# Strassen's seven products for the first feed-forward product of a decoder layer

## The chip, the core and the metric

The kernel runs on one core of a Trainium2 chip: TensorE (PE) for matrix products, VectorE (DVE), ScalarE (ACT) and GpSimd (POOL) for elementwise work, SyncE (SP) for issuing the transfers between DRAM and the on-chip memory SBUF. Products land in PSUM, which has eight banks of 512 fp32 columns. The metric is the device time of one execution in microseconds (us), the median of several runs.

## The reference, cut to what matters

One decoder layer on 512 tokens of width 2048: an attention mixer, then the feed-forward part, then a gate with a per-layer embedding, and a last norm. The change is in the feed-forward part (and in how all weights from there on are staged).

```python
h = h + nsa_mixer(rms_norm(h, norm_mix[i]), ...)
hn = rms_norm(h, norm_ffn[i])                            # 512 x 2048
h = h + jnp.square(jax.nn.relu(hn @ ffn_w1[i])) @ ffn_w2[i]   # 2048 -> 8192 -> 2048
gate = jax.nn.sigmoid(rms_norm(h, norm_ple[i]) @ ple_w_gate[i])
h = h + (p[i] @ ple_w_proj[i]) * gate
return rms_norm(h, norm_final)
```

## The kernel before

All is kept transposed: features on the 128 partitions, the 512 tokens along the columns. `h` is 16 tiles of 128 x 512, held in SBUF from start to end.

**Precision.** Each fp32 operand is split in an upper part (fp16) and a lower part (the rest, fp16), and each product is three matmuls (`mm3`, L68): upper by upper, upper by lower, lower by upper. Every matmul (L66) is preceded by its weight load. Since fp16 has a small range, each weight unit is scaled by a power of two first.

**Weight units.** From the feed-forward part on, weights come in units of 128 x 2048 fp32 (1 MB). `unit16` (L687) loads one on SP's queue, sums its squares on ACT (`sum_sq`, L676, whose unwanted elementwise result goes into the buffer of the lower part, L692), takes the power of two (`scale_of`, L666: one 128x1 matmul to bank `s1`, then three tiny DVE operations, L671 to L673), and splits it by halves of 1024 columns (`scaled_split`, L680: upper on ACT, L684; lower on DVE, L685). Five split units fit (`w16`), and raw ones in three buffers (`rawt`, L79). `take(n, ahead)` (L711) hands out the next units and prepares four more ahead.

**Feed-forward.** 8192 inner features are 16 groups G of four blocks of 128. `up(G)` (L838) makes a group: for each block, one weight unit, 16 values of k, 3 matmuls of 512 columns into one bank (`gemm16`, L826), then relu and scale on DVE (L848), square on ACT (L850) and a sum of the squares for the next scale (L851). `squash` (L857) scales and splits the group's result. `down(G)` (L872) multiplies it by four units of the second weight, 4 x 4 output tiles of 4 x 3 matmuls each, and adds each to `h` on DVE (L883). The order is up 0, up 1, down 0, up 2, down 1, and so on. Four banks rotate (`gbank`, L785).

**Ahead of it** `norm_late` (L215) gives the norm's factor, `proj(0)` (L792) computes half of the embedding's projection into eight tiles `pj` that stay in SBUF until the gate, and `normed` (L807) scales and splits `h` into `xs`: per k one DVE scaling (L812), the upper part on ACT (L815), the lower on DVE (L816). `take_held` (L822) holds the next units back until the tenth k is split. **Behind it** come `proj(1)`, `normed` again, 16 gate units of the same shape (the last two by token halves, so by matmuls of 256 columns, L938), the last norm and the output tiles `fo` (L953).

**Order.** Instructions are written down in program order, and a planner orders each engine's queue when the program is built, with its own estimate of the times; on the chip every queue then runs strictly in that order, each instruction waiting for what it needs.

Of the kernel before, what the change touches and what calls it, by code (L numbers as in the profile page):

```python
# [7 lines left out]
F32 = mybir.dt.float32  # L8
# [20 lines left out]
HOLD = 9  # L29
EPS = 1e-6  # L30
# [6 lines left out]
def trunk_kernel(ctx, tc, xT, pT, gains, w_kcvc, w_blk, w_gates, w_out, w1c, w2c, posT,  # L37
# [8 lines left out]
    wraw = ctx.enter_context(tc.tile_pool(name="wraw", bufs=2))  # L46
    tmp = ctx.enter_context(tc.tile_pool(name="tmp", bufs=2))
    a_sb = ctx.enter_context(ExitStack())
    wsp = a_sb.enter_context(tc.tile_pool(name="wsp", bufs=3))
# [29 lines left out]
    def rawt(shape=(128, 2048), own=False):  # L79
        rawt.n += 1  # L80
        if own or (rawt.mix and rawt.n % 3 == 0):
            return P["raw2"].tile(list(shape), F32, name="raw", tag="raw")
        return wraw.tile(list(shape), F32, name="raw", tag="raw")

    rawt.n = 0
    rawt.mix = False
    P = {}

    def load(src, cols=2048, pieces=1, own=False):
        r = rawt(own=own)  # L90
# [575 lines left out]
    def scale_of(sq, n=1):  # L666
        p = bank("s1")
        mm(p[:, 0:n], wb[:, 0:128], sq, True, True)
# [18 lines left out]
    def unit16(src):  # L687
        r = load(src, own=not rawt.mix)
        hi = P["w16"].tile([128, 2048], F16, name="wh", tag="wh")
        lo = P["w16"].tile([128, 2048], F16, name="wl", tag="wl")  # L690
        sq = P["sm"].tile([128, 1], BF16, name="sq", tag="sq")
        sum_sq(lo.bitcast(BF16), r, sq)  # L692
        sc, inv = scale_of(sq)
        scaled_split(hi, lo, r, sc)
        return hi, lo, inv

    order = [w_proj[0]]
    for G in range(NG + 1):
        if G < NG:
            order += [ffn1[G * FG + j] for j in range(FG)]  # L700
        if G > 0:
            order += [ffn2[G - 1, c] for c in range(4)]
    order += [w_proj[1]] + [w_pg[m] for m in range(NK)]
    units = []
    taken = [0]

    def prep(n):
        while len(units) < min(len(order), n):
            units.append(unit16(order[len(units)]))

    def take(n=1, ahead=4):  # L711
        taken[0] += n
        prep(taken[0] + ahead)
        return units[taken[0] - n:taken[0]]

    def embed_in():
        px = [P["px"].tile([128, 2 * S], F16, name=f"px{e}", tag=f"px{e}") for e in range(2)]
        praw = load(pT, 1024, own=True)
        sqp = P["sm"].tile([128, 1], BF16, name="sq", tag="sq")
        sum_sq(px[1].bitcast(BF16), praw[:, 0:1024], sqp)  # L720
        psc, pinv0 = scale_of(sqp)
        P["pinv"] = pinv = P["keepc"].tile([128, 1], F32, name="pinv")
        DVE.tensor_copy(pinv, pinv0)
        scaled_split(px[0], px[1], praw[:, 0:1024], psc)
        P["pxs"] = px

    def early(n0, n1, gains=False):
        if gains:
            embed_in()
            yield  # L730
            gain_scales()
            yield
        for n in range(n0, n1):
            prep(n + 1)
            yield
# [18 lines left out]
    for hd in range(HEADS):  # L754
# [8 lines left out]
        elif hd + 2 < HEADS:  # L763
            merge([(pvg, 10), (s_stage(hd + 1, (pp, small)), 5)], n, fill)
        elif hd + 1 < HEADS:
            merge([(pvg, 10), (s_stage(hd + 1, (pp, small)), 5), (early(0, 1, True), 3)], n, fill)
        else:
            merge([(pvg, 10), (early(1, 3), 2)], n, fill)
        if hd == HEADS - 3:
            x_sb.close()  # L770
            for nm, bufs in (("sm", 6), ("keepc", 1), ("px", 1), ("w16", 5), ("raw2", 1)):
# [3 lines left out]
    merge([(early(3, 4), 2)], 16, fill)  # L775
    drain(fill)
    a_sb.close()
    rawt.mix = True
    pjp = pool("pjp")
    xp = pool("xp", side="left")  # L780
    wk = pool("wk", 4, side="left")
# [10 lines left out]
    def proj(q):  # L792
        hi, lo, inv = take(1, 3)[0]
        px = P["pxs"]
        iv = P["sm"].tile([128, 1], F32, name="iv", tag="iv")
        DVE.tensor_mul(iv, inv, P["pinv"])
        for m in range(8):
            o = gbank()
            for e in range(2):
                ws = slice(e * 1024 + m * 128, e * 1024 + (m + 1) * 128)  # L800
                xs = slice(e * S, (e + 1) * S)
                mm3(o, hi[:, ws], lo[:, ws], px[0][:, xs], px[1][:, xs], e == 0, e == 1)
            t = pjp.tile([128, S], F32, name="pj", tag=f"pj{q * 8 + m}")
            ACT.activation(t, o, AF.Copy, scale=iv)
            pj.append(t)

    def normed(i, rs):  # L807
        gx = P["gx"]
        xs = []
        for k in range(NK):  # L810
            t = wk.tile([128, S], F32, name="xt", tag="t")
            DVE.scalar_tensor_tensor(t, h[k], gx[:, i, k:k + 1], rs, op0=OP.mult, op1=OP.mult)  # L812
            a = xp.tile([128, S], F16, name="xh", tag=f"xh{k}")
            b = xp.tile([128, S], F16, name="xl", tag=f"xl{k}")
            ia = ACT.activation(a, t, AF.Copy)  # L815
            ib = DVE.tensor_sub(b, t, a)  # L816
            if k == HOLD:
                held[:] = ia, ib
            xs.append((a, b))
        return xs  # L820

    def take_held(n):  # L822
        with tc.issue_after(held[0].ins), tc.issue_after(held[1].ins):
            return take(n, 3)

    def gemm16(os, us, xs):  # L826
        for k in range(NK):
            for o, (hi, lo, _) in zip(os, us):
                ws = slice(k * 128, (k + 1) * 128)
                mm3(o, hi[:, ws], lo[:, ws], xs[k][0], xs[k][1], k == 0, k == NK - 1)  # L830
# [4 lines left out]
    with tc.tile_pool(name="ff", bufs=1) as ff:  # L835
        xs = normed(0, rs)

        def up(G, prev=None):  # L838
            fq = P["sm"].tile([128, FG], F32, name="fq", tag="fq")
            fj = ff.tile([128, S], BF16, name="fj", tag="fj")  # L840
            ts = []
            for j0, step in (((0, 2), (2, 1), (3, 1)) if G == 0 else ((0, 1), (1, 1), (2, 1), (3, 1))):
                us = take_held(step) if step == 2 else take(step)
                os = [gbank() for _ in us]
                gemm16(os, us, xs)
                for j, (o, u) in enumerate(zip(os, us), j0):
                    t = wk.tile([128, S], F32, name="ft", tag="t")
                    DVE.tensor_scalar(t, o, 0.0, u[2], op0=OP.max, op1=OP.mult)  # L848
                    t2 = ff.tile([128, S], F32, name="ft2", tag=f"t2{j}")
                    ACT.activation(t2, t, AF.Square)  # L850
                    ACT.activation(fj, t2, AF.Square, accum_out=fq[:, j:j + 1])  # L851
                    ts.append(t2)
                if prev and j0 == 0:
                    sqd.append(squash(*prev))
            return ts, fq
# [16 lines left out]
        def down(fs, fiv, last, prev=None):  # L872
            for c in range(4):
                hi, lo, inv = take()[0]
                iv = P["sm"].tile([128, 1], F32, name="iv", tag="iv")
                DVE.tensor_mul(iv, inv, fiv)
                for e in range(4):
                    m = 4 * c + e
                    o = gbank()
                    for j in range(FG):  # L880
                        ws = slice(j * 512 + e * 128, j * 512 + (e + 1) * 128)
                        mm3(o, hi[:, ws], lo[:, ws], fs[j][0], fs[j][1], j == 0, j == FG - 1)
                    DVE.scalar_tensor_tensor(h[m], o, iv, h[m], op0=OP.mult, op1=OP.add)  # L883
                    if last:
                        norm_sq(m, 12)
# [147 lines left out]
```

## Time and profile before

| | us |
|---|---|
| median of 3 runs | 2403.87 (2402.72 to 2404.31) |
| the profiled execution | 2402.69 |
| its span, first to last instruction | 2400.6 |
| TensorE busy in the span | 2367.3 (99%) |
| VectorE busy | 1303.8 (54%) |
| ScalarE busy | 1128.5 (47%) |
| mean granted clock of TensorE | 0.994 of full |

The span is one execution, and the rest of the profiled time lies around it. Busy time of TensorE says little by itself, since matmuls overlap: the listed duration of a 512-column matmul is about 380 ns, the distance from one start to the next about 216 ns. In the feed-forward part the kernel runs in groups that repeat every 83.10 us.

### The profile page before, as it was taken

How to read it: one execution, taken by the hardware profiler on the slowest of the kernel's cores; microseconds unless marked ns; L12 is line 12 of the kernel's file. 1: busy time of each engine (PE TensorE's matmuls, PEld its weight loads, DVE VectorE, ACT ScalarE, POOL GpSimd, SP SyncE). 2: the span in 40 equal slices, each digit the busy share in tenths (PEclk: the TensorE clock that was granted, in tenths of full speed). 3: DMA queues.
4: the chain of work that ended last, by engine and by line, in shares of the span. 5: the costliest groups of instructions: out<-in, count | busy, mean ns of one | idle time of the engine just before them, and what ended most of it. 6: DMA issues, size and time to landing. Idle time of an engine off the chain costs nothing.

```text
span 2400.6 us, 28596 instructions
## 1 busy us (share of the span) xinstructions
PE 2367.3 (99%) x11495; PEld 1406.4 (59%) x11495; DVE 1303.8 (54%) x2410; ACT 1128.5 (47%) x1638; POOL 328.9 (14%) x176
## 2 busy tenths in 40 slices
PE   8999999999999989999999999999999999999997
PEld 6888888888888744444444444444444444444445
DVE  6347656656556864554455445545544544555643
ACT  5324333333334566545445444544454454545751
POOL 4253233333323210000000000000000000002012
PEclk9999999999999999999999999999999999999998
DMA  5232122222222323323332233222332233322311
GB/s 196 95 123 71 53 71 71 71 71 71 71 71 79 123 71 123 104 90 106 106 106 90 103 105 106 97 98 104 106 105 95 100 105 105 102 92 88 108 69 71
DMA packets 35557, 227.35 MB, mean 95 GB/s; under 512 B 4320, under 2 KB 4704, under 8 KB 9568
## 3 DMA queue, kind: packets, MB, share of 16 engines
q1 hardware_dynamic: 35424, 225.53, 27.2%
q8 instruction: 90, 1.47, 0.3%
q14 instruction: 43, 0.35, 0.0%
HBM read 221.32 MB, written 4.19 MB: 94 GB/s over the span
## 4 chain that ended last, share of the span: by engine, by line
PE 96%; DVE 2%; issue 1%; ACT 0%; POOL 0%; DMA 0%; SPq 0%; DVEq 0%; POOLq 0%; ACTq 0%
PE g_ps L66 54%; PE pt_ps L66 32%; PE s_ps L66 5%; PE o_ps L66 3%; PE pt_ps L430 1%; DVE h L302 0%; DVE wl L685 0%; PE pt_ps L422 0%; DVE p L387 0%; DVE xt L812 0%; POOL raw L962 0%; DMA h<-in_xT_dram 0%; DVE al L168 0%; DVE nm L374 0%; DVE raw L964 0%
## 5 line engine op out<-in xcount | busy, mean ns | idle before, releaser
L66 PEld LDWEIGHTS <-wh 128*128 128x128 f16 x4736 | 461.9, 98 | 546.9 <-issue 6.6
L684 ACT ACTIVATE wh<-raw,sc 128x1024 f16<-128x1024 f32 x292 | 319.3, 1140 | 459.6 <-DVE sc L672 459.6
L685 DVE SCALAR_TENSOR_TENSOR wl<-raw,sc,wh 128x1024 f16<-128x1024 f32 x292 | 367.4, 1285 | 131.6 <-ACT wh L684 131.6
L66 PEld LDWEIGHTS <-wl 128*128 128x128 f16 x2368 | 231.5, 98 | 259.7 <-issue 3.9
L678 ACT ACTIVATE wl<-raw 128x2048 bf16<-128x2048 f32 x146 | 278.6, 1908 | 205.0 <-PE g_ps L66 123.6
L75 POOL TENSOR_TENSOR wl<-raw,wh 128x1024 fp32r<-128x1024 f32 x100 | 240.6, 2411 | 507.0 <-ACT wh L74 497.1
L182 POOL TENSOR_TENSOR ssacc<-ssacc,sq 128x512 f32<-128x512 f32 x50 | 73.8, 1477 | 1493.3 <-issue 1342.3
L66 PE MATMUL pt_ps<-xl,wh 128*128 128x512 f16 (+1 forms) x672 | 252.1, 375 | 2.2 <-DVE xl L816 2.2
L66 PE MATMUL pt_ps<-xh,wh 128*128 128x512 f16 (+1 forms) x672 | 249.8, 375 | 3.0 <-ACT xh L815 3.0
L66 PE MATMUL pt_ps<-xh,wl 128*128 128x512 f16 (+1 forms) x672 | 252.2, 375 | 0.0
L66 PE MATMUL g_ps<-xh,wh 128*128 128x512 f16 (+1 forms) x640 | 239.4, 374 | 0.0
L66 PE MATMUL g_ps<-xh,wl 128*128 128x512 f16 (+1 forms) x640 | 239.3, 374 | 0.0
L66 PE MATMUL g_ps<-xl,wh 128*128 128x512 f16 (+1 forms) x640 | 239.3, 374 | 0.0
L74 ACT ACTIVATE wh<-raw 128x1024 fp32r<-128x1024 f32 (+1 forms) x122 | 125.6, 1043 | 223.3 <-PE g_ps L66 159.7
L671 DVE TENSOR_SCALAR e<-s_ps 128x1 int32<-128x1 int32 x164 | 25.5, 155 | 354.1 <-PE s_ps L66 346.9
L66 PE MATMUL g_ps<-ah,wh 128*128 128x512 f32 x544 | 215.2, 396 | 0.0
L66 PE MATMUL g_ps<-ah,wl 128*128 128x512 f32 x544 | 214.0, 394 | 0.0
L66 PE MATMUL g_ps<-al,wh 128*128 128x512 f32 x544 | 212.7, 391 | 0.0
L883 DVE SCALAR_TENSOR_TENSOR h<-pt_ps,iv,h 128x512 f32<-128x512 f32 x128 | 96.0, 750 | 180.7 <-PE pt_ps L66 180.7
L66 PE MATMUL pt_ps<-fh,wl 128*128 128x512 f16 x512 | 194.0, 379 | 0.0
L66 PE MATMUL pt_ps<-fl,wh 128*128 128x512 f16 x512 | 194.0, 379 | 0.0
L66 PE MATMUL pt_ps<-fh,wh 128*128 128x512 f16 x512 | 194.0, 379 | 0.0
(243 smaller groups left out, 3627.0 us busy)
## 6 DMA issues: line engine op xcount, KB each, us to landing
raw<-in_ffn_dram SPq DMA_DIRECT2D x128, 1024.0 KB, 4.9
raw<-in_w_blk_dram SPq DMA_DIRECT2D x32, 1024.0 KB, 4.9
raw<-in_w_out_dram SPq DMA_DIRECT2D x16, 1024.0 KB, 4.8
raw<-in_w_pg_dram SPq DMA_DIRECT2D x16, 1024.0 KB, 4.9
h<-in_xT_dram SPq DMA_DIRECT2D x16, 256.0 KB, 6.6
raw<-in_w_kcvc_dram SPq DMA_DIRECT2D x4, 1024.0 KB, 4.9
raw<-in_w1c_dram SPq DMA_DIRECT2D x4, 1024.0 KB, 5.6
raw<-in_w_kcvc_dram SPq DMA_DIRECT2D x6, 512.0 KB, 6.6
```

The source lines that it names most:

```text
L66: nc.tensor.matmul(o, w, x, start=start, stop=stop, skip_group_check=True)
L74: ACT.activation(hi, src, AF.Copy)
L75: (eng or DVE).tensor_sub(lo, src, f32(hi))
L182: (DVE if e else POOL).tensor_add(acc[e], acc[e], sq)
L430: nc.tensor.transpose(pt[:, (i - kc) * 128:(i - kc + 1) * 128], A["P", hd, b, i, kc], ident)
L671: DVE.tensor_scalar(e[:, 0:n], p[:, 0:n].bitcast(I32), 24, None, op0=OP.logical_shift_right)
L678: ACT.activation(junk, src, AF.Square, accum_out=sq)
L684: ACT.activation(hi[:, cs], src[:, cs], AF.Copy, scale=sc)
L685: DVE.scalar_tensor_tensor(lo[:, cs], src[:, cs], sc, hi[:, cs], op0=OP.mult, op1=OP.subtract)
L883: DVE.scalar_tensor_tensor(h[m], o, iv, h[m], op0=OP.mult, op1=OP.add)
```

## The change

Blocks of the first feed-forward product are taken two at a time from group 2 on (`STD = 2`). The pair's weight (256 output features x 2048), the input (2048 x 512 tokens) and the result are each cut in 2 x 2 blocks, and the eight block products of the plain scheme are replaced by seven (Strassen's scheme in Winograd's form): each is 8 values of k, 3 matmuls, 256 columns. For that,

- `combos(k)` makes four sums of blocks of the input once, during groups 0 and 1, which stay on the plain scheme but with matmuls of 256 columns;
- `prepare` makes four sums of weight blocks for each pair (S1 to s4, on DVE), and splits seven pieces, not four;
- `up_pair` runs the products over four banks x, v, y, u; two banks take a second product on top of the first, after ACT has copied the first sum out (`keep`) or DVE has used it (`total`).

Weights are staged in pieces of 1024 columns: six raw buffers, nine slots of split pieces. `pump` is called after every product (`used`), stages a unit when its raw buffers are free by count, and splits one piece when a slot is free. Squares go quarter by quarter, with the unwanted result in PSUM, and `scale_of` sums the columns by one tiny matmul each. The first half of the projection is written to DRAM (`pjd`) and read back before the gate; the embedding is loaded and split twice. Buffers of the working tiles `wk` go from four to three, those of `fo` from three to two.

```diff
+RAWS = 6
+SLOTS = 9
+STD = 2
+H2 = S // 2
...
-        mm(p[:, 0:n], wb[:, 0:128], sq, True, True)
+        c = sq.shape[-1] // n
+        for x in range(c):
+            mm(p[:, 0:n], wb[:, 0:128], sq[:, x * n:(x + 1) * n], x == 0, x == c - 1)
...
+    PAIR = ("11", "12", "S2", "S1", "s3", "22", "s4")
+
+    def stage(it):
+        it.raw = []
+        if len(it.src) == 2:
+            quarters = [(it.src[a], b) for a, b in ((0, 0), (1, 0), (1, 1), (0, 1))]
+        else:
+            quarters = [(it.src[0], b) for b in range(need(it))]
+        ps4 = P["sm"].tile([128, 4], BF16, name="sq4", tag="sq4")
+        for x, (src, b) in enumerate(quarters):
+            r = P["raw"].tile([128, 1024], F32, name="raw", tag="raw")
+            nc.sync.dma_start(out=r, in_=src[:, b * 1024:(b + 1) * 1024])
+            sum_sq(sbank()[:, 0:1024], r, ps4[:, x:x + 1])
+            it.raw.append(r)
+        it.sc, it.inv = scale_of(ps4[:, 0:len(quarters)])
+
+    def slot(it, name, src):
+        hi = P["w16"].tile([128, 1024], F16, name="wh", tag="wh")
+        lo = P["w16"].tile([128, 1024], F16, name="wl", tag="wl")
+        scaled_split(hi, lo, src, it.sc)
+        it.w[name] = (hi, lo)
+
+    def prepare(it):
+        if len(it.src) == 1:
+            for b in range(need(it)):
+                slot(it, b, it.raw[b])
+                yield
+            return
+        a11, a21, a22, a12 = it.raw
+        for name in PAIR:
+            if name == "S2":
+                s1 = P["S"].tile([128, 1024], F32, name="S1", tag="S")
+                s2 = P["S"].tile([128, 1024], F32, name="S2", tag="S")
+                DVE.tensor_add(s1, a21, a22)
+                DVE.tensor_add(s2, s1, a11)
+            elif name == "s3":
+                s3 = P["S"].tile([128, 1024], F32, name="S3", tag="S")
+                DVE.tensor_add(s3, a11, a21)
+            elif name == "s4":
+                DVE.tensor_add(s2, s2, a12)
+            slot(it, name, {"11": a11, "12": a12, "22": a22}.get(name) or
+                 {"S2": lambda: s2, "S1": lambda: s1, "s3": lambda: s3, "s4": lambda: s2}[name]())
+            yield
+
...
+            items += [Item(ffn2[G - 1, c]) for c in range(4)]
+    items += [Item(pT), Item(w_proj[1])] + [Item(w_pg[m]) for m in range(NK)]
...
+    def pump():
+        while True:
+            n = st["staged"]
+            if n < min(len(items), st["limit"]) and st["raws"] + need(items[n]) <= RAWS:
+                stage(items[n])
+                st["raws"] += need(items[n])
+                st["staged"] += 1
+                continue
+            n = st["split"]
+            if n < st["staged"] and st["slots"] < SLOTS:
+                if st["gen"] is None:
+                    st["gen"] = prepare(items[n])
+                    st["left"] = 7 if need(items[n]) == 4 else need(items[n])
+                next(st["gen"])
+                st["slots"] += 1
+                st["left"] -= 1
+                if need(items[n]) == 4:
+                    st["raws"] -= {2: 2, 1: 1, 0: 1}.get(st["left"], 0)
+                else:
+                    st["raws"] -= 1
+                if st["left"] == 0:
+                    next(st["gen"], None)
+                    st["gen"] = None
+                    st["split"] += 1
+                continue
+            return
+
+    def used():
+        st["slots"] -= 1
+        pump()
+
...
+            for nm, bufs in (("sm", 12), ("keepc", 1), ("w16", SLOTS), ("raw", RAWS)):
...
+    P["S"] = pool("S", 2, side="left")
+    wk = pool("wk", 3, side="left")
+    pjd = tc.dram_tile([8, 128, S], F32, name="pjd")
...
+            else:
+                t = wk.tile([128, S], F32, name="pjt", tag="t")
+                ACT.activation(t, o, AF.Copy, scale=iv)
+                nc.sync.dma_start(out=pjd[m], in_=t)
+        for e in range(3):
+            used()
...
+    def held_pump(limit):
+        with tc.issue_after(held[0].ins), tc.issue_after(held[1].ins):
+            st["limit"] = limit
+            pump()
...
+                wh, wl = it.w[k // 8]
+                ws = slice(k % 8 * 128, (k % 8 + 1) * 128)
+                for x, (c0, n) in enumerate(widths):
+                    xh, xl = xs[k][x]
+                    mm3(o[:, c0:c0 + n], wh[:, ws], wl[:, ws], xh, xl, k == 0 and x == 0, k == NK - 1)
+            if k % 8 == 7:
+                for _ in its:
+                    used()
...
+            if k < 8:
+                a = [xp.tile([128, H2], F16, name=f"x1{c}", tag=f"x1{c}{k}") for c in "hl"]
+                b = [keep12[c][k // 2][:, k % 2 * H2:(k % 2 + 1) * H2] for c in range(2)]
+                xsplit(a[0], a[1], t[:, 0:H2])
+                xsplit(b[0], b[1], t[:, H2:])
+                xs.append([tuple(a), tuple(b)])
+                X["11", k] = tuple(a)
...
+        def combos(k):
+            ta, tb = xt(0, k, rs), xt(0, k + 8, rs)
+            cm = P["S"].tile([128, 4, H2], F32, name="cm", tag="S")
+            DVE.tensor_sub(cm[:, 0], ta[:, 0:H2], ta[:, H2:])
+            DVE.tensor_sub(cm[:, 2], tb[:, H2:], ta[:, H2:])
+            DVE.tensor_add(cm[:, 3], cm[:, 0], tb[:, H2:])
+            DVE.tensor_sub(cm[:, 1], cm[:, 3], tb[:, 0:H2])
+            a = [xp.tile([128, 4, H2], F16, name=f"xc{c}", tag=f"xc{c}{k}") for c in "hl"]
+            xsplit(a[0][:, 0:3], a[1][:, 0:3], cm[:, 0:3])
+            ACT.activation(a[0][:, 3], cm[:, 3], AF.Copy, scale=-1.0)
+            DVE.scalar_tensor_tensor(a[1][:, 3], cm[:, 3], -1.0, a[0][:, 3], op0=OP.mult, op1=OP.subtract)
+            for x, n in enumerate(("t1", "T4", "T3", "t2")):
+                X[n, k] = (a[0][:, x], a[1][:, x])
+
+        def squares(c, fq, j, ts):
+            t2 = ff.tile([128, S], F32, name="ft2", tag=f"t2{j}")
+            ACT.activation(t2, c, AF.Square)
+            sum_sq(sbank()[:, 0:S], t2, fq[:, j:j + 1])
+            ts.append(t2)
+
...
+        def up_pair(G, j0, fq, ts, hook):
+            it = take()
+            ninv = P["sm"].tile([128, 1], F32, name="ninv", tag="ninv")
+            DVE.tensor_scalar(ninv, it.inv, -1.0, None, op0=OP.mult)
+            z = {}
+            c = [wk.tile([128, S], F32, name="ft", tag="t") for _ in range(2)]
+            o = {}
+
+            def prod(b, w, x, first):
+                if first:
+                    o[b] = gbank()
+                wh, wl = it.w[w]
+                for k in range(8):
+                    ws = slice(k * 128, (k + 1) * 128)
+                    xh, xl = X[x, k]
+                    mm3(o[b][:, 0:H2], wh[:, ws], wl[:, ws], xh, xl, first and k == 0, k == 7)
+
+            def keep(n):
+                z[n] = wk.tile([128, H2], F32, name="z", tag="z")
+                ACT.activation(z[n], o["x"][:, 0:H2], AF.Copy)
+
+            def total(e, half, n, b):
+                DVE.tensor_add(c[e][:, half * H2:(half + 1) * H2], z[n], o[b][:, 0:H2])
+
+            prod("x", "11", "11", True)
+            keep(1)
+            used()
+            prod("v", "12", "21", True)
+            total(0, 0, 1, "v")
+            used()
+            prod("x", "S2", "t2", False)
+            keep(2)
+            used()
+            prod("y", "S1", "t1", True)
+            used()
+            hook(G, j0)
+            prod("x", "s3", "T3", False)
+            keep(3)
+            total(1, 1, 3, "y")
+            used()
+            prod("u", "22", "T4", True)
+            total(1, 0, 3, "u")
+            used()
+            prod("y", "s4", "22", False)
+            total(0, 1, 2, "y")
+            used()
+            for e in (1, 0):
+                DVE.tensor_scalar(c[e], c[e], ninv if e else it.inv, 0.0, op0=OP.mult, op1=OP.max)
+            for e in range(2):
+                squares(c[e], fq, j0 + e, ts)
...
+                if G == 0 and j0 >= 2:
+                    combos(j0 - 2)
+                if G == 1 and j0 < 3:
+                    combos(2 + 2 * j0)
+                    combos(3 + 2 * j0)
+
+            if G < STD:
+                up_std(G, fq, ts, hook)
+            else:
+                for j0 in (0, 2):
+                    up_pair(G, j0, fq, ts, hook)
...
+    P["pj"] = pool("pjp", side="left")
     proj(1)
+    xp = pool("xp2", side="left")
+    for m in range(8):
+        t = P["pj"].tile([128, S], F32, name="pj", tag=f"pj{m}")
+        nc.sync.dma_start(out=t, in_=pjd[m])
+        pj.insert(m, t)
...
-                fo = rawt((128, 8, HT))
+                fo = plx.tile([128, 8, HT], F32, name="fo", tag="fo")
```

## Rows read from the trace of the kernel before

**Rows 1.** The page: busy time by engine, and the chain's shares.
```profile
PE 2367.3 (99%) x11495; PEld 1406.4 (59%) x11495; DVE 1303.8 (54%) x2410; ACT 1128.5 (47%) x1638; POOL 328.9 (14%) x176
...
PE 96%; DVE 2%; issue 1%; ACT 0%; POOL 0%; DMA 0%; SPq 0%; DVEq 0%; POOLq 0%; ACTq 0%
```

**Rows 2.** Stretches: length, busy us (instructions) by engine, clock, DMA; group 1's up units; a steady group.
```profile
912.80:954.40 41.60, 41.60 (x199) 18.92 (x197) 19.39 (x38) 24.17 (x32) 0.00 (x0) 1.00 0.32 110
...
1079.10:1162.20 83.10, 83.10 (x394) 37.77 (x393) 40.77 (x74) 40.95 (x48) 0.00 (x0) 1.00 0.30 102
```

**Rows 3.** The chain in order of time: start, us, what, count; 512-column, then 256-column matmuls.
```profile
1085.12 10.38 PE pt_ps L66 x48
...
2361.89 10.49 PE g_ps L66 x96
```

**Rows 4.** Timeline of TensorE (start, us, instruction) around one scale matmul.
```profile
900.50 0.38 PE L66 MATMUL g_ps<-xl,wh 128*128 128x512 f16 x1
900.72 0.17 PE L66 MATMUL s_ps<-sq,wb 128*128 128x1 bf16 x1
900.75 0.38 PE L66 MATMUL g_ps<-xh,wl 128*128 128x512 f16 x1
```

**Rows 5.** Groups by line and shape, whole span: count, busy us, mean ns, idle before.
```profile
L66 PEld LDWEIGHTS <-wh 128*128 128x128 f16 x4736 | 461.9, 98 | 546.9 <-issue 6.6
L685 DVE SCALAR_TENSOR_TENSOR wl<-raw,sc,wh 128x1024 f16<-128x1024 f32 x292 | 367.4, 1285 | 131.6 <-ACT wh L684 131.6
L684 ACT ACTIVATE wh<-raw,sc 128x1024 f16<-128x1024 f32 x292 | 319.3, 1140 | 459.6 <-DVE sc L672 459.6
L678 ACT ACTIVATE wl<-raw 128x2048 bf16<-128x2048 f32 x146 | 278.6, 1908 | 205.0 <-PE g_ps L66 123.6 <-PE pt_ps L66 51.1 <-PE s_ps L66 27.8
...
L850 ACT ACTIVATE ft<-ft 128x512 f32<-128x512 f32 x64 | 39.1, 612 | 0.0
...
L812 DVE SCALAR_TENSOR_TENSOR xt<-h,gx,o_ps 128x512 f32<-128x512 f32 x32 | 22.4, 742 | 4.5 <-PE o_ps L66 4.5
...
L816 DVE TENSOR_TENSOR xl<-xt,xh 128x512 f16<-128x512 f32 x32 | 20.9, 685 | 2.3 <-ACT xh L815 2.3
...
L75 DVE TENSOR_TENSOR tl<-pt_ps,th 128x256 fp32r<-128x256 f32 x32 | 13.4, 418 | 21.7 <-ACT th L74 21.7
```

**Rows 6.** Waits over the span: who waited for whom, us, times, longest.
```profile
DVE e L671 <- PE s_ps L66: 346.9, 71, 5.3
...
DVE wl L685 <- ACT wh L684: 131.6, 126, 3.3
```

**Rows 7.** Timelines of ScalarE and TensorE: one unit's square, accumulator, scale matmul, upper half.
```profile
1079.11 1.91 ACT L678 ACTIVATE wl<-raw 128x2048 bf16<-128x2048 f32 x1 [1.74 <-PE g_ps L66]
1080.93 0.19 ACT L678 ACTIVATION_READ_ACCUMULATOR wl<-raw 128x1 bf16 x1
...
1084.95 0.17 PE L66 MATMUL s_ps<-sq,wb 128*128 128x1 bf16 x1
...
1085.57 2.19 ACT L684 ACTIVATE wh<-raw,sc 128x1024 f16<-128x1024 f32 x2 [4.46 <-DVE sc L672]
```

**Rows 8.** Timelines of ScalarE and VectorE where the feed-forward part begins.
```profile
863.20 0.69 ACT L804 ACTIVATE pj<-g_ps,iv 128x512 f32<-128x512 f32 x1 [1.41 <-PE g_ps L66]
...
865.64 2.72 DVE L812 SCALAR_TENSOR_TENSOR xt<-h,gx,o_ps 128x512 f32<-128x512 f32 x4 [1.31 <-PE o_ps L66]
```

**Rows 9.** DMA issues: count, KB each, median us from issue to landing.
```profile
raw<-in_ffn_dram SPq DMA_DIRECT2D x128, 1024.0 KB, 4.9
...
out_dram<-raw SPq DMA_DIRECT2D x3, 256.0 KB, 2.6
```

**Rows 10.** Timelines of GpSimd and VectorE at the output tiles.
```profile
2382.95 5.20 POOL L962 TENSOR_TENSOR raw<-h,r 128x256 f32<-128x256 f32 x7 [4.22 <-ACT r L948]
...
2391.25 4.39 DVE L964 TENSOR_TENSOR raw<-h,s_ps 128x256 f32<-128x256 f32 x13 [1.31 <-PE s_ps L66]
```

More of the change, by code (lines that the diff above doesn't have):

```diff
@@ L77, in trunk_kernel, with load @@
     lo_eng = [DVE]
[L79 to L86, printed above, removed]
     P = {}
-    def load(src, cols=2048, pieces=1, own=False):
-        r = rawt(own=own)
+    def load(src, cols=2048, pieces=1):
+        r = wraw.tile([128, 2048], F32, name="raw", tag="raw")
         n = cols // pieces
@@ L685, in scaled_split @@
             DVE.scalar_tensor_tensor(lo[:, cs], src[:, cs], sc, hi[:, cs], op0=OP.mult, op1=OP.subtract)
[L687 to L695, printed above, removed]
@@ L698, in trunk_kernel @@
+    items = [Item(pT), Item(w_proj[0])]
+    seq = {}
     for G in range(NG + 1):
         if G < NG:
-            order += [ffn1[G * FG + j] for j in range(FG)]
+            ms = [ffn1[G * FG + j] for j in range(FG)]
+            seq["up", G] = len(items)
+            items += [Item(a) for a in ms] if G < STD else [Item(*ms[0:2]), Item(*ms[2:4])]
         if G > 0:
-            order += [ffn2[G - 1, c] for c in range(4)]
-    order += [w_proj[1]] + [w_pg[m] for m in range(NK)]
-    units = []
@@ L705, in trunk_kernel @@
[L705 to L725, printed above, removed]
+            items += [Item(ffn2[G - 1, c]) for c in range(4)]
@@ L822, in take_held @@
[L822 to L830, printed above, removed]
+                mm3(o, wh[:, ws], wl[:, ws], px[0][:, xs], px[1][:, xs], e == 0, e == 1)
+            if q:
+                t = P["pj"].tile([128, S], F32, name="pj", tag=f"pj{8 + m}")
+                ACT.activation(t, o, AF.Copy, scale=iv)
+                pj.append(t)
+            else:
+                t = wk.tile([128, S], F32, name="pjt", tag="t")
+                ACT.activation(t, o, AF.Copy, scale=iv)
+                nc.sync.dma_start(out=pjd[m], in_=t)
@@ L838, in up, with hook @@
         def up(G, prev=None):
             fq = P["sm"].tile([128, FG], F32, name="fq", tag="fq")
-            fj = ff.tile([128, S], BF16, name="fj", tag="fj")
             ts = []
[L842 to L852, printed above, removed]
+            def hook(G, j0):
@@ L918, in trunk_kernel @@
         while m < NK - NL:
-            us = take_held(2) if m == 0 else take(1)
+            us = [take() for _ in range(2 if m == 0 else 1)]
             os = [gbank() for _ in us]
+            if m == 0:
+                held_pump(len(items))
             gemm16(os, us, xs)
@@ L926, in trunk_kernel @@
                 m += 1
-        kept = [(u, gate_inv(u)) for u in take(NL)]
+        kept = [(u, gate_inv(u)) for u in (take() for _ in range(NL))]
         rfs = []
```

128 lines of the change are left out of this document (83 added, 45 removed).

## The prediction

> **What bounds the kernel now.** I read the page first: TensorE is busy 99% of the span and 96% of the chain that ended last is TensorE [rows 1]. Then the table by stage: one steady group of the feed-forward part (four up units, four down units) takes 83.10 us, TensorE is busy for all of it at full clock, VectorE (DVE) for 40.8 us and ScalarE (ACT) for 40.95 us [rows 2]. So in the stretch that is changed TensorE is the bound, and the other two have half of their time free. What a matmul costs there is its spacing and not its listed duration: 48 products of 512 columns take 10.38 us in the chain, 216.25 ns each; 96 products of 256 columns, in the last stage, take 10.49 us, 109.3 ns each [rows 3]. That pair of numbers carries the forecast.
>
> **The change part by part.**
>
> *Pairs, groups 2 to 15.* Before, two up units are 2 x 16 x 3 = 96 matmuls of 512 columns: 96 x 216.25 ns = 20.76 us. After, seven products of 8 x 3 = 24 matmuls of 256 columns: 168 x 109.3 ns = 18.36 us. Saved: 2.40 us a pair, 4.80 us a group, with 14 groups 67.2 us. No stall of TensorE is listed in a steady group, so all of it lies on the path.
>
> A half-width matmul gives its weight load only half the cover: the load's mean is 98 ns [rows 5] against a spacing of 109.3. The row decides, since those 96 products have a load each and still keep 109.3 ns; at 512 columns the spacing is 216 and not 98 more. The Trainium skill, page "TensorE: Matmul & The Clock Gate", section "The mechanism", speaks against this: a load overlaps a running matmul only if it goes to another group of array rows, and here each load takes all the rows. It is a rival below.
>
> *Groups 0 and 1* stay standard, but in halves: 768 x 109.3 - 384 x 216.25 ns = +0.9 us, on the path.
>
> *Scale matmuls.* Each quarter of a weight now has its own column of the sum of squares, so a scale takes four tiny matmuls (pair) or two (others), not one. One costs 34 ns of TensorE: the neighbours of the one at 900.72 start 0.25 us apart and not 0.216 [rows 4]. A group had 9 and gets 2 x 4 + 4 x 2 + 1 = 17: +0.27 us, 14 times 3.8 us. The rest (8 standard, 8 further down, 16 gate, 2 projection units, one embedding again) is about 35 more, 1.2 us. As the tiny ones stand in a row, each could cost as much as the 98 ns of its load; that would add 147 x 64 ns = 9.4 us. I take 34 ns, the row of the same instruction.
>
> *VectorE in a steady group.* Pairs need 14 splits, not 8: 6 x 1.285 = 7.7 us more. Weight sums: 4 a pair, 1024 columns fp32. From 512 columns at 685 ns and 256 at 418 the slope is 1.04 ns a column, so 1.22 us (an estimate), times 8 = 9.8. The four sums of products (256 columns, 0.42 us) of each pair: 3.4. All [rows 5]. 40.8 + 20.9 + 0.3 for the negated scale = 62.0 us of the new group.
>
> *ScalarE in a steady group.* Six more upper halves: 6 x 1.14 = 6.8. Squares by quarters: 512 columns take 0.61, 2048 take 1.91 us [rows 5], 1024 thus 1.04, with 0.19 for the accumulator [rows 7]; 16 x 1.23 - 8 x 2.10 = 2.9. Six copies of 256 columns at about 0.40 (same slope): 2.4. Sum 53.1 us. The new group is 83.10 - 4.80 + 0.27 = 78.6 us, so VectorE stands at 79% and ScalarE at 68%: all of this hides, by the mean. Within a pair's 18.4 us the next pair needs 7 x 1.285 + 4 x 1.22 = 13.9 of VectorE and the sums and the relu about 3.2; ScalarE 4 x 1.23 + 7 x 1.14 + 3 x 0.40 + 2 x 1.43 = 17.0. It just fits, and nine slots are at least 18 us of lead, so a slot that comes late by some us costs nothing. Without that cover each late slot costs its lateness.
>
> *New short waits.* This is what the trace of before doesn't show. Bank x is read by the copy before the next product adds to it: the cover is one product, 2.62 us. The copy takes 0.2 + 0.40 us, so 2.0 us remain for what stands ahead of it on ScalarE; one split (1.14) fits. Bank y is tighter: the copy of the fifth product, then the sum on VectorE (0.42) and two hand-overs, about 1.1 us of 2.62; 1.5 remain, and one instruction ahead on each engine (1.14 and 1.285) makes 2.4. Behind the waiting matmul stands all of TensorE. Bounds per pair: 0 and about 1.0 us. Both engines are at work about half of the time together (0.68 x 0.79); I take 0.35, nearer to nothing, as the planner can set a ready product first. 28 x 0.35 = 9.8 us.
>
> *Combinations of x*, in groups 0 and 1: per k two scaled rows (2 x 0.74), four sums (4 x 0.42), a lower half of 768 columns (0.95) and one of 256 (0.43): 4.5 us of VectorE, eight times 36 us. Group 1's up units use 19.4 of 41.6 us [rows 2]; six combinations make that 46.4, so VectorE falls some 5 us behind. The lead of nine slots is 47 us of standard work: cost nothing; bare, 5 us.
>
> *Splitting x.* For k < 8 two lower halves of 256 replace one of 512: 8 x (2 x 0.418 - 0.685) = 1.2 us on VectorE. TensorE can use the third ready unit meanwhile, so nothing; at most 1.2.
>
> *Projection through DRAM.* Its eight tiles take three buffers that the scaled x needs next. The last copy ends at 863.9; a 256 KB write lands 2.6 us after issue [rows 9], so 866.5, and the third x tile starts at 865.64 + 1.4 = 867.0 [rows 8]: just hidden, bound 0 to 2 us. The writes stand on SP's queue, where no weight load is due before the hold. The loads back stand there ahead of the third gate unit, which is needed two units (20.8 us) later, against about 10 us for 2 MB at the rate of 1 MB in 4.9 us [rows 9]: nothing; bare, up to 10. The embedding's second split costs half a unit of the free engines.
>
> *Ring of the output tiles*: two, not three. The first tile's last write starts when its last multiply ends, about 2386, and lands by 2389; the third tile is written from 2391.25 [rows 10]: nothing, bound 2 us.
>
> **Sum.** 67.2 - 0.9 - 3.8 - 1.2 = 61.3 us off, 9.8 back: 51.5. The profiled execution took 2402.7 us (span 2400.6 and 2.1 around it), so 2351.2; the median is 1.2 higher: 2352.
>
> **The rivals.**
>
> *A. ScalarE stands at a square that waits for its DMA.* Before, the square's junk went into the lower half's buffer, so a square ran only when TensorE had freed that buffer [rows 7], long after landing; no square waited for data. Now the junk goes to PSUM and the square can reach the head of the queue before its quarter is there, and the copies that TensorE waits for are behind it. If that happens once a group, for the landing of 4.9 us [rows 9] less the 2.0 us of cover, it costs 2.9 x 14 = 41 us: 2393. For it: six quarter buffers, of which a pair takes four. Against it: the order is planned with the loads in it, and DMA is 30% busy [rows 2].
>
> *B. VectorE becomes the bound (the slower side).* It waited 346.9 us for scale matmuls and 131.6 for upper halves [rows 6], over 146 units, that is 18.25 groups: 26.2 us a group. If those waits stay beside 62.0 us of work, a group takes 88.2 us, 5.1 more than before: 14 x 5.1 = 71, so 2475. It decides from 21 us of waits a group (83.1 - 62.0). For it: TensorE's scale matmul comes 3.8 us after the square is done, and ScalarE stood 4.46 us for it with nothing done [rows 7]; both queues are in order, and the weight sums add a to and fro between them. Against it: these are waits of queues with nothing else to do, and most could be filled.
>
> *C. Weight loads in the open.* By that section of the page each of 168 loads would add its 98 ns: 16.5 us a pair, 28 pairs 461 us: about 2810. [Rows 3] exclude it but for a change of pattern. That the change isn't seven products is excluded by the diff.
>
> **How the numbers follow.** Forecast 0.64 (its own range 2340 to 2371: no stall and a little gained at the start, up to 1.0 us a pair), A 0.18 (2371 to 2410), B 0.17, C 0.01. Range 2340 to 2400 leaves out B, C and the end of A, 2 in 10. A measurement of this kernel tells about 0.2% (4.8 us) from no change: faster is the forecast and most of A, 0.64 + 0.13 = 0.77; same 0.03; slower 0.02 + 0.17 + 0.01 = 0.20.
>
> **What the profile after would show.** Right: steady groups of about 79 us at full clock, a spacing of 109 ns in the products, VectorE near 62 and ScalarE near 53 us in them, and small idle times of TensorE, released by the copies and by the sums of products. A: ScalarE's squares idle before a weight DMA. B: TensorE idle before upper or lower halves of weights, VectorE near 100% or its waits still at 26 us a group. C: a spacing near 200 ns. A group above 83 us would prove the forecast wrong; one under 78.3 would mean that an added matmul costs less than I count.

## The result and the profile after

The changed kernel takes 2377.1 us (median of 4; 2375.3 to 2378.5) against 2404.1 us: ratio 0.9888, interval 0.9871 to 0.9905. That is 27 us faster, about half of the 51.5 us forecast. Its profiled span is 2374.7 us, against 2400.6 before.

The page first: busy time of each engine, then the chain's shares.

```profile
PE 2314.3 (97%) x14042; PEld 1642.1 (69%) x14042; DVE 1570.0 (66%) x2737; ACT 1289.7 (54%) x2125; POOL 327.2 (14%) x176
...
PE 72%; DMA 10%; ACT 8%; DVE 6%; issue 3%; SPq 0%; POOL 0%; ACTq 0%; DVEq 0%; POOLq 0%
```

Against [rows 1], TensorE is busy 53 us less, so the products did get shorter. But it is no longer alone on the chain: a tenth of that is now DMA, and ScalarE (ACT) has 8% of it. The table by stage places this. It shows one steady group (window, length, busy us by engine, clock, DMA):

```profile
1050.59:1131.62 81.03, 79.38 (x547) 52.02 (x545) 57.56 (x92) 51.26 (x76) 0.00 (x0) 1.00 0.32 105
```

The group of [rows 2] took 83.10 us, all of it busy. This one takes 81.03, with 1.65 us in which TensorE stands by its listed times; a listed matmul outlasts its spacing and so covers a part of each stop. From the starts of the first down product of each group, the steady groups are 81.27 us long on average, where the forecast without stalls had 78.6. That comparison gives the loss.

To count lost time I took the gaps between starts of successive matmuls and subtracted the spacing of their kind (0.216, 0.109 and 0.034 us). The feed-forward part has 31.4 us of such gaps at scale matmuls and 9.8 us at matmuls that wait for a copy out of PSUM. It lasts 1310.1 us against 1333.6, measured from the first product with x to the last down product. It begins 2.2 us earlier (864.9 against 867.1), and what follows it, to the end of the span, is as long as before (199.7 and 200.0).

The waits of the whole span (who waited for whom, us, times, longest) say who is late. TensorE's are listed idle times, shorter than the gaps above:

```profile
ACT s_ps L676 <- DMA raw<-in_ffn_dram: 200.3, 122, 4.4
PE s_ps L70 <- ACT s_ps L676: 21.6, 42, 1.9
...
PE pt_ps L70 <- ACT z L976: 7.3, 14, 1.1
```

L676 is the square of a quarter. Before, the squares waited for TensorE [rows 5]; now 122 of them wait for a feed-forward weight's DMA. TensorE then waits for the square at the scale matmul (second line) and for the copies `z` of a product's sum (third line). Each run's kernel has its own line numbers: here L676 is the square and L976 the copy. The timeline shows one such place (start, us, instruction, idle before and its releaser):

```profile
1107.39 1.28 DVE L683 SCALAR_TENSOR_TENSOR wl<-raw,sc,wh 128x1024 f16<-128x1024 f32 x1
...
1108.70 3.43 SPq L701 DMA_DIRECT2D raw<-in_ffn_dram  x2
...
1113.33 1.03 ACT L676 ACTIVATE s_ps<-raw 128x1024 f32<-128x1024 f32 x1 [1.47 <-DMA raw<-in_ffn_dram]
...
1114.39 1.13 ACT L682 ACTIVATE wh<-raw,sc 128x1024 f16<-128x1024 f32 x1
1114.54 0.16 PE L70 MATMUL s_ps<-sq,wb 128*128 128x1 bf16 x1 [0.49 <-ACT s_ps L676]
1115.43 0.36 ACT L976 ACTIVATE z<-pt_ps 128x256 f32<-128x256 f32 x1
1115.84 0.38 PE L70 MATMUL pt_ps<-fh,wh 128*128 128x512 f16 x1 [0.47 <-ACT z L976]
```

A load is issued at 1108.70, and the square that reads it starts at 1113.33, after ScalarE has stood 1.47 us with nothing else to do. Everything behind the square in ScalarE's queue is late: an upper half at 1114.39 and the copy z at 1115.43. TensorE pays twice, at the scale matmul and at the matmul that needs z's bank. The chain at that place is the same story (start, us, what):

```profile
1107.39 0.07 DVE wl L683
1107.45 1.14 issue
1108.59 0.11 DVE iv L1047
1108.70 4.55 DMA raw<-in_ffn_dram
...
1113.33 0.07 ACT s_ps L676
...
1114.54 0.16 PE s_ps L70
```

VectorE's lower half of 1107.39, by these times the last reader of a quarter's old contents, lasts until 1108.67 (the chain names iv, the tiny step right behind it). The load leaves at 1108.70, and the 4.55 us until it has landed lie on the chain.

### The profile page after: what moved, and what is told of

It is laid out like the page before. It is cut to its first block, busy times and chain, and to the rows that moved or that the text cites. A ratio compares the mean times of both kernels' runs of the same rounds, so it can differ in the third digit from the quotient of the medians.

```text
span 2374.7 us, 35228 instructions
## 1 busy us (share of the span) xinstructions
PE 2314.3 (97%) x14042; PEld 1642.1 (69%) x14042; DVE 1570.0 (66%) x2737; ACT 1289.7 (54%) x2125; POOL 327.2 (14%) x176
## 4 chain that ended last, share of the span: by engine, by line
PE 72%; DMA 10%; ACT 8%; DVE 6%; issue 3%; SPq 0%; POOL 0%; ACTq 0%; DVEq 0%; POOLq 0%
PE g_ps L70 43%; PE pt_ps L70 20%; DMA raw<-in_ffn_dram 9%; PE s_ps L70 5%; ACT wh L682 4%; ACT s_ps L676 3%; PE o_ps L70 3%; DVE wl L683 2%; PE pt_ps L426 1%; DMA h<-in_xT_dram 1%; DVE ft L979 0%; DVE xt L873 0%; DVE S L727 0%; PE pt_ps L418 0%; DVE p L383 0%
## 5 line engine op out<-in xcount | busy, mean ns | idle before, releaser
L70 PEld LDWEIGHTS <-wh 128*128 128x128 f16 x6336 | 611.2, 98 | 362.7 <-issue 36.6
L70 PEld LDWEIGHTS <-wl 128*128 128x128 f16 x3168 | 309.5, 98 | 181.9 <-issue 12.4
L676 ACT ACTIVATE s_ps<-raw 128x1024 f32<-128x1024 f32 x294 | 301.1, 1024 | 228.9 <-DMA raw<-in_ffn_dram 200.3
L70 PE MATMUL pt_ps<-fh,wh 128*128 128x512 f16 (+1 forms) x544 | 202.8, 373 | 7.3 <-ACT z L976 7.3
L70 PE MATMUL pt_ps<-fl,wh 128*128 128x512 f16 (+1 forms) x544 | 202.9, 373 | 0.0
L70 PE MATMUL pt_ps<-fh,wl 128*128 128x512 f16 (+1 forms) x544 | 202.9, 373 | 0.0
L70 PE MATMUL g_ps<-fh,wh 128*128 128x512 f16 (+1 forms) x544 | 202.8, 373 | 0.0
L70 PE MATMUL g_ps<-fh,wl 128*128 128x512 f16 (+1 forms) x544 | 202.7, 373 | 0.0
L70 PE MATMUL g_ps<-fl,wh 128*128 128x512 f16 (+1 forms) x544 | 202.6, 373 | 0.0
L683 DVE SCALAR_TENSOR_TENSOR wl<-S,sc,wh 128x1024 f16<-128x1024 f32 x112 | 143.4, 1281 | 85.6 <-ACT wh L682 85.6
L682 ACT ACTIVATE wh<-S,sc 128x1024 f16<-128x1024 f32 x112 | 128.0, 1142 | 70.1 <-PE pt_ps L70 38.9
```

Source lines behind the costliest of these rows:

```text
L70: nc.tensor.matmul(o, w, x, start=start, stop=stop, skip_group_check=True)
L676: ACT.activation(junk, src, AF.Square, accum_out=sq)
L682: ACT.activation(hi[:, cs], src[:, cs], AF.Copy, scale=sc)
L683: DVE.scalar_tensor_tensor(lo[:, cs], src[:, cs], sc, hi[:, cs], op0=OP.mult, op1=OP.subtract)
```

## The experiments

First theory, T: the ring of six quarter buffers is too small. A load is issued only when a buffer comes free, lands late, and TensorE loses the time at the scale matmuls. Its rivals were that the stall lies in the order of the queues, whatever the ring (P); that it comes from staging by quarters and has nothing to do with the pairs (S); and that VectorE or ScalarE is short of time (B). This table has all ten runs. "Feed-forward" runs from the first product with x to the last down product; "gaps" are the two sums named above, scale matmuls and copies.

| run | median us | before, same chip | ratio (interval) | feed-forward us | gaps us |
|---|---|---|---|---|---|
| before | 2404.1 | | | 1333.6 | |
| after | 2377.1 | 2404.1 | 0.9888 (0.9871 to 0.9905) | 1310.1 | 31.4 + 9.8 |
| e1_raw8 | 2363.5 | 2403.1 | 0.9834 (0.9820 to 0.9849) | 1300.7 | 14.2 + 16.6 |
| e2_fixscale | 2381.5 | 2403.1 | 0.9911 (0.9896 to 0.9926) | 1309.8 | 0 + 40.0 |
| e3_std16 | 2425.3 | 2403.1 | 1.0091 (1.0076 to 1.0106) | 1358.4 | 15.4 + 0 |
| e4_raw8_fixscale | 2362.6 | 2403.1 | 0.9829 (0.9812 to 0.9845) | 1298.6 | 0 + 24.0 |
| e5_resident | 2339.3 | 2401.5 | 0.9743 (0.9728 to 0.9757) | 1269.2 | 0 + 0.3 |
| e6_late_squares | 2338.9 | 2401.5 | 0.9737 (0.9723 to 0.9752) | 1271.3 | 1.9 + 0 |
| e7_late_squares_raw8 | 2335.4 | 2401.5 | 0.9722 (0.9708 to 0.9737) | 1269.6 | 0 + 0.3 |
| e8_late1_raw8 | 2336.1 | 2401.5 | 0.9729 (0.9713 to 0.9746) | 1270.0 | 1.0 + 0.3 |
| e9_late_scale_only | 2375.3 | 2402.4 | 0.9894 (0.9878 to 0.9911) | 1309.9 | 34.1 + 6.0 |
| e10_late_squares_only | 2338.5 | 2402.4 | 0.9734 (0.9719 to 0.9748) | 1271.6 | 1.5 + 0.2 |

**e1: two more quarter buffers.**

```diff
+    P["raw2"] = pool("raw2", 2, side="left")
...
-            r = P["raw"].tile([128, 1024], F32, name="raw", tag="raw")
+            r = rawt()
...
-            if n < min(len(items), st["limit"]) and st["raws"] + need(items[n]) <= RAWS:
+            if n < min(len(items), st["limit"]) and st["raws"] + need(items[n]) <= RAWS + (2 if "raw2" in P else 0):
```

`rawt` deals the tiles out over six old and two new buffers in turn.

> Two more raw buffers of 1024 columns from the feed-forward part on (eight, not six); all else as after. Theory T (a raw buffer comes free late, so its load lands late, so the square on ScalarE is late, and TensorE stands at the scale matmul, 1.9 us a group, or at the copy behind such a square, 0.6 us a group): loads are issued earlier by some us, most of the 2.5 us a group goes, 14 groups: 2377 - 30 = about 2347, group of 78.8 to 79.3 us. Rival P (the planner puts scale matmuls as early as it believes loads to land, whatever the number of buffers): it moves them earlier too, 2370 to 2380. Rival B (VectorE or ScalarE are short of time): the waits move to weights, above 2368.

It gains some 13 us, 9.4 of them in the feed-forward part, and so lies between T's 2347 and rival P's 2370. The waits show why (same columns; the first line is ScalarE's):

```profile
ACT s_ps L676 <- DMA raw<-in_ffn_dram: 203.3, 103, 4.2
PE pt_ps L70 <- ACT z L986: 13.7, 13, 2.4
PE s_ps L70 <- ACT s_ps L676: 12.1, 15, 1.7
```

The waits at scale matmuls fall from 42 to 15, while those at copies grow from 7.3 to 13.7 us, and ScalarE stands at squares as long as before (203.3 against 200.3 us). The ring is a part of the cause and no more.

**e2: the scale matmuls read a constant.** Squares and loads are all kept; the scale is a fixed power of two for each kind of weight, so TensorE waits for no square there.

```diff
-        it.sc, it.inv = scale_of(ps4[:, 0:len(quarters)])
+        it.sc, it.inv = scale_of(P["fix", it.kind][:, 0:len(quarters)])
```

> As after, but each scale matmul reads a constant tile in place of the sums of squares, so it waits for no square; squares, loads, scale matmuls and splits are all still done. Left out: the scale no longer depends on the data. Theory T: the 1.9 us a group in which TensorE stands at scale matmuls goes, the 0.6 us at the copy may stay: 2377 - 26 = about 2351, group of 79.2 us. Rival B (ScalarE and VectorE are what is short, and the scale matmul only the place where it shows): TensorE waits for split weights in its place, above 2368.

T fails here. Its 31 us at scale matmuls are gone, and the feed-forward part is as long as before the edit (1309.8 against 1310.1). Rival B's time (above 2368) came, but not its waits for split weights. The median is 4 us worse although that part is no longer: it starts 7.3 us later, at 872.2. In e4 and e5, which have the same constant, it starts 7.6 and 4.6 us later; no run shows why, so these three are best compared by the column of the feed-forward part. The waits of TensorE:

```profile
PE pt_ps L70 <- ACT z L984: 35.0, 28, 2.8
```

And ScalarE's squares by line, in a stretch as long as a steady group (1049 to 1130 us; count, busy us, mean ns, idle before and its releaser):

```profile
L676 ACT ACTIVATE s_ps<-raw 128x1024 f32<-128x1024 f32 x17 | 17.4, 1026 | 12.8 <-DMA raw<-in_ffn_dram 12.4
```

It is the same time in another place: 28 waits at copies, on an engine that stands 12.4 us a group at squares.

**e3: all sixteen groups plain,** in halves but with the new staging by quarters. No pairs.

```diff
-STD = 2
+STD = 16
```

> All 16 groups by the plain scheme in halves (no pairs, no weight sums; the combinations of x are still made), with the new staging. Price of the staging and halves alone. Theory T: a slot lasts 5.2 us in place of 2.6, so six raw buffers do, and no wait for squares: before 2404 + 16 x 0.44 for half-width matmuls + about 5 for the added scale matmuls = 2416. Rival S (the staging by pieces itself makes TensorE wait, with pairs or without): some 2 us a group more, 2440.

```profile
ACT s_ps L676 <- DMA raw<-in_ffn_dram: 541.9, 232, 5.0
PE s_ps L70 <- ACT s_ps L676: 11.6, 21, 1.4
```

The result lies between the two expectations. The new staging alone makes TensorE wait at scale matmuls (15.4 us of gaps), without any pair. With the pairs, which have copies behind the squares, the gaps are more than twice that. ScalarE stands 541.9 us at squares here, far more than in the changed kernel, and TensorE loses less: how long a queue stands is not what it costs.

**e4: e1 and e2 together.** The scale is a constant here too.

```diff
+    P["raw2"] = pool("raw2", 2, side="left")
...
-        it.sc, it.inv = scale_of(ps4[:, 0:len(quarters)])
+        it.sc, it.inv = scale_of(P["fix", it.kind][:, 0:len(quarters)])
```

> e1 and e2 together: eight raw buffers and scale matmuls that wait for nothing. Left out: the scale no longer depends on the data. Theory T: nothing is left to wait for, group of 78.2 to 78.8 us: about 2342, and no more than some us under e1. Rival P: clearly under e1 and near e2. Rival B: above 2360.

T's 2342 is missed by 20 us, 7.6 of them by the later start. Rival B's bound (above 2360) is met, as in e2; e5 decides against it. The profiled execution was the longest of the four, 8.8 us above the median, so its lengths are rough; its gaps, 24.0 us, are at copies:

```profile
PE pt_ps L70 <- ACT z L994: 20.7, 14, 3.4
```

After these four, T2 replaced T: ScalarE's queue stands at a square whose load has not landed, and TensorE pays wherever it next needs ScalarE. If so, the same number of squares costs nothing when none waits for data, and neither the ring nor the scale matmul has to change.

**e5: squares of a resident tile.** Each square reads a tile that stays in SBUF, not its quarter, and the scale is a constant. The work on every engine stays; only the wait for the load goes. Against e2 only the tile that is read differs.

```diff
-            sum_sq(sbank()[:, 0:1024], r, ps4[:, x:x + 1])
+            sum_sq(sbank()[:, 0:1024], P.get("still", r), ps4[:, x:x + 1])
...
-        it.sc, it.inv = scale_of(ps4[:, 0:len(quarters)])
+        it.sc, it.inv = scale_of(P["fix", it.kind][:, 0:len(quarters)])
```

> As after, but from the feed-forward part on each square reads a resident tile in place of the weights just loaded, and the scale matmul a constant tile: ScalarE does the same work, but none of its squares waits for a load. Left out: the scale no longer depends on the data. Theory T2 (formed from e1 and e2: what TensorE loses is ScalarE's in-order queue standing at a square whose load has not landed; it shows at the scale matmul or, if that is freed, at the copies): both kinds of stall go, group 78.8 to 79.3 us, 2377 - 32 = about 2345. Rival B (ScalarE and VectorE have too much work in a pair's stretch): TensorE still loses 2 us a group, above 2368.

```profile
1049.00:1128.00 79.00, 79.00 (x549) 52.26 (x547) 57.99 (x94) 52.00 (x77) 0.00 (x0) 1.00 0.31 107
```

TensorE is busy for all of the 79 us window, with the same work beside it (ScalarE 52.0 us, VectorE 58.0). Steady groups take 78.55 us, and the feed-forward part is 40.6 us shorter than in e2. So it is the standing and not the work.

**e6: the squares later, with all of the work left in.** A weight's loads are issued as before; its squares are queued two products later and ordered behind the last split or copy on ScalarE, its scale matmuls one product after that and ordered on TensorE.

```diff
             nc.sync.dma_start(out=r, in_=src[:, b * 1024:(b + 1) * 1024])
-            sum_sq(sbank()[:, 0:1024], r, ps4[:, x:x + 1])
...
+    def square(it):
+        with after("act"):
+            for x, r in enumerate(it.raw):
+                sum_sq(sbank()[:, 0:1024], r, it.ps4[:, x:x + 1])
...
+    def scale(it):
+        with after("pe"):
+            it.sc, it.inv = scale_of(it.ps4)
...
+            if n < st["staged"] and (not lag or st["clock"] - items[n].at >= 2):
+                square(items[n])
...
+            if n < st["squared"] and (not lag or st["clock"] - items[n].at2 >= 1):
+                scale(items[n])
```

`after` wraps what it encloses in `tc.issue_after` of that last instruction; `st["clock"]` counts products, and `lag` is on in the steady groups.

> Six raw buffers as after, same work, but in the steady groups a unit's squares are written two products after its loads and ordered behind the last split or copy on ScalarE, and its scale matmul one product later still, behind that product on TensorE. Theory T2: the order is the fault; the queues no longer stand: 2345 to 2355. Against it: with six buffers a longer hold of each makes loads later, and split weights come late (rival B'): above 2365 with waits of TensorE for weights.

The ring is still six quarters, and rival B' (weights come late) does not show. The feed-forward part is 62.3 us shorter than before the change; the forecast's sum without stalls was 61.3. The groups of ScalarE by line, within one steady group, first after, then e6 (count, busy us, mean ns, idle before and its releaser):

```profile
L676 ACT ACTIVATE s_ps<-raw 128x1024 f32<-128x1024 f32 x16 | 16.4, 1026 | 13.2 <-DMA raw<-in_ffn_dram 13.1
```

```profile
L679 ACT ACTIVATE s_ps<-raw 128x1024 f32<-128x1024 f32 x16 | 16.2, 1014 | 0.1
```

The same sixteen squares; 13.1 us of standing a group became 0.1.

**e7 and e8: both remedies.** e7 is e6 with the eight buffers of e1. e8 is e7 with the squares one product after the loads and not two:

```diff
-            if n < st["staged"] and (not lag or st["clock"] - items[n].at >= 2):
+            if n < st["staged"] and (not lag or st["clock"] - items[n].at >= 1):
```

> e6 with eight raw buffers. Theory T2: the stalls go and the longer hold is paid by the two buffers: group 78.8 to 79.5 us, 2343 to 2352, under e1 (2363). Rival B: as e1 or above.

> As e7, but the squares come one product after the loads and not two. Theory T2: between e1 and e7, as a load takes 3.7 us and a product 2.6: 2347 to 2358.

e7 is the fastest full kernel, 2335.4 us, 66 us under the kernel before. The ring adds 3.5 us to what the order gives, with intervals that overlap, and 1.7 us in the feed-forward part. With eight buffers one product of delay does as well as two; with six, one was not run. e5 to e8 came out 6 to 11 us under their forecasts (the low ends, where there is a range): their steady groups last 78.55 to 78.57 us, where the forecasts that name a length had 78.8 and more.

**e9 and e10: which half of e6 does it.** e9 delays only the scale matmuls (squares queued with the loads), e10 only the squares (the scale matmul right behind them, not ordered on TensorE). The cuts, e9's and then e10's, are against e6; e9 also drops the order on ScalarE.

```diff
-            if n < st["staged"] and (not lag or st["clock"] - items[n].at >= 2):
+            if n < st["staged"] and (not lag or st["clock"] - items[n].at >= 0):
...
-            if n < st["squared"] and (not lag or st["clock"] - items[n].at2 >= 1):
+            if n < st["squared"] and (not lag or st["clock"] - items[n].at2 >= 2):
```

```diff
-            if n < st["squared"] and (not lag or st["clock"] - items[n].at2 >= 1):
+            if n < st["squared"] and (not lag or st["clock"] - items[n].at2 >= 0):
```

> As after (six buffers, squares at their old place), but in the steady groups the scale matmul is written two products after the squares and ordered behind that product on TensorE. Theory T2 (the queue that stands is ScalarE's): TensorE no longer waits at scale matmuls, but at the copies behind a square without data, as in e2: 2368 to 2382. Rival Q (TensorE's own queue is the fault, ScalarE's order would do): 2338 to 2350.

> As after, but in the steady groups only the squares are put two products later and behind the last split or copy on ScalarE; the scale matmul follows at once, with no order on TensorE. Theory T2: waits at copies go; waits at scale matmuls shrink, since a square now starts with its data there, but one that the planner sets too early may stay: 2339 to 2356. Rival Q: no better than 2365.

The squares' row in one steady group, e9 and then e10:

```profile
L679 ACT ACTIVATE s_ps<-raw 128x1024 f32<-128x1024 f32 x16 | 16.4, 1026 | 13.7 <-DMA raw<-in_ffn_dram 13.5
```

```profile
L679 ACT ACTIVATE s_ps<-raw 128x1024 f32<-128x1024 f32 x16 | 16.2, 1015 | 0.1
```

e10 alone has all of e6's gain; e9 alone has none of it. So ScalarE's order settles it. In e9 I had expected the waits to move to the copies. They did not (its line of waits):

```profile
PE s_ps L72 <- ACT s_ps L679: 24.7, 45, 1.2
```

The later scale matmul is still the first to meet a standing ScalarE; why it is that one here, and the copies in e2, no run settles.

## Why the prediction was right or wrong

- *What bounds the kernel, and the pairs:* right. With the standing taken away (e5, e6), a steady group takes 78.55 us; the sum without stalls had 78.6. That covers the 67.2 us for the pairs, the 34 ns of a scale matmul (the 98 ns bound is excluded: it would add about 0.5 us a group) and the half-width spacing at once.
- *Rival C, weight loads in the open:* refuted. The chain of e6 has two whole products (start, us, what):

```profile
1084.10 2.62 PE g_ps L72 x24
1086.72 2.62 PE pt_ps L72 x24
```

24 half-width matmuls in 2.62 us are 109.2 ns each, each with a load of its own. The rule of the Trainium skill ("TensorE: Matmul & The Clock Gate", section "The mechanism"), as I read it in the forecast, does not hold for these loads, which take all the rows. The same section of the Trainium skill names a second case, a load into the background weight buffer, which I left out; no run here shows by which way these loads are hidden.
- *Rival B, VectorE:* refuted. In e5 VectorE works 58.0 us of 79 and TensorE never stands, so its waits for scale matmuls and upper halves were idle time that could be filled. My 62.0 was high for three reasons. The two relus of a pair read SBUF and take 0.48 us where they took 0.75 from PSUM (1.1 us a group). A group has seven scales and not nine (0.9 us). And I added listed durations to a busy time, though the records of neighbours overlap: over 13 steady groups the durations add up to 62.4 us a group and cover 57.6 (before, 43.5 and 40.8). The single prices held:

```profile
L727 DVE TENSOR_TENSOR S<-raw 128x1024 f32<-128x1024 f32 x28 | 34.2, 1220 | 0.5
L979 DVE TENSOR_TENSOR ft<-z,g_ps 128x256 f32<-128x256 f32 x84 | 32.5, 414 | 2.8 <-PE g_ps L70 2.7
L976 ACT ACTIVATE z<-pt_ps 128x256 f32<-128x256 f32 x84 | 30.7, 366 | 35.9 <-PE pt_ps L70 35.9
```

1220 ns against an estimate of 1.22 us, 414 against 0.42, 366 against 0.40. ScalarE came to 51.3 us a group; my 53.1 was too high mostly by the same adding.
- *New short waits:* this is the step that failed. I took 0.35 us a pair, 9.8 us in all, with bounds of 0 and 1.0. Measured: (81.27 - 78.55) x 14 = 38 us, or 1.36 us a pair, past the upper bound. I had priced what stands ahead of a copy as one more busy instruction (a split of 1.14 us). What stood there was a queue with nothing to do, waiting for a DMA. And the wait at the scale matmul, three quarters of the gaps, was priced nowhere in my sum.
- *Rival A* named that mechanism, at (4.9 - 2.0) x 14 = 41 us, close to the 38 measured. The mechanism was right, the size was luck: A had one wait a group of 4.9 us, of which TensorE loses 2.9, and the steady group above has ten waits of ScalarE, 13.1 us, of which TensorE loses about 2.5 in several short stops. A should have stood in place of the 9.8 us and not on top of them: 2402.7 - 61.3 + 41 = 2382, against 2376.5 in the profiled execution. The range 2340 to 2400 held the result because it took in most of A; the forecast's own range, 2340 to 2371, did not. I put it second for a bad reason: that DMA is 30% busy. A low share says nothing of when a load may start; here it starts when a buffer is freed, and 4.55 us later the square may run.
- *Why hardly any square waited before:* nearly as said under A; two of them did wait for a weight's DMA, 2.5 us in all. The junk of a square went into a buffer that TensorE freed, so a wait for TensorE [rows 7] hid the landing. Sending the junk to PSUM took that brake away, and e6 puts a brake back. That it was the junk's place, and not another part of the new staging, is argued from these rows: no run puts the junk back. e3 shows only that with the new staging squares wait for their loads even without pairs.
- *Steps costed at nothing:* right as a whole. The feed-forward part begins 2.2 us earlier, and what follows it takes 199.7 us against 200.0, so projection, gate loads and output ring cost nothing there. One copy of the projection did wait for a write to DRAM, 0.68 us, with no delay at the start.

Open: why the order made for ScalarE puts squares ahead of their landing, since what it assumes of landing times is in no trace.

## What to carry to other kernels

When a change frees an instruction from an old wait, ask what that wait was hiding: in an in-order queue the instruction now stands at its next unmet condition, and everything behind it stands too. A wait of TensorE names its last releaser and not the cause; freeing the place where it shows (e2) moves it to the next one, so follow the chain to the engine that stands with nothing done. Queue an instruction that needs a load a product or two after that load: in e10, with two, this took 38 us off the feed-forward part, with no buffer added and no work changed.

## What the runs showed that I had not expected

- Taking away the wait that made three quarters of TensorE's lost time gained nothing (feed-forward 1309.8 against 1310.1 us): another wait in the shadow of the same square took its place.
- Two more buffers gave about a third (13 us; in the feed-forward part 9.4 of 38.5), the order of one queue all of it. The Trainium skill, "Perfetto Trace Analysis", section "Optimization Strategy", says that gaps which repeat on the engine that should be full can mean too few buffers. These gaps repeat in each group, and the runs agree with that reading only in part: e10 closes them with the six buffers that were there.
- ScalarE stood 13.1 us a group at squares and TensorE lost only 2.5 to 2.7 of it; in e3, without pairs, ScalarE stood 541.9 us in all and TensorE lost 15.4. That the cover of one product (2.62 us with pairs, about 5.2 in a plain group) took up the rest is how I read it; no run isolates it.
